# A hybrid Conformer and attention step: attention and convolution put in source order on VectorE and ScalarE, key, value and state loads issued early, first and last transfers in parts

## The chip, the cores and the metric

The kernel runs on one core of one Trainium2 chip. The core has a matmul engine (PE, with its weight loads PEld), a vector engine (DVE), a scalar engine (ACT), GpSimd (POOL), a sync engine (SP) that issues most transfers, and 16 DMA engines that carry them. In the trace each engine takes its instructions in the order in which they stand in the built program; one at the head that waits holds all behind it. The metric is the device time of one execution in microseconds (us), lower is better.

## What is computed

One layer of a streaming encoder, for 256 rows of a new sequence and 8 running streams of 16 rows, 384 rows in all, in float32:

```python
h    = rmsnorm(x, norm_mix_g)
proj = h @ w_in                  # glu | q | k | v | forget logits | gate_a | gate_b
u    = glu_in[..., :D_CONV] * sigmoid(glu_in[..., D_CONV:])
z    = layernorm(causal_dwconv(ext, conv_dw_w, conv_dw_b), conv_ln_g, conv_ln_b)   # 31 taps
a_out = (z * sigmoid(z)) @ conv_pw_out
logf = log_sigmoid(f_logit + b_forget)
b_out = attn_fn(rmsnorm(q, q_norm_g), rmsnorm(k, k_norm_g), v, logf) @ w_att_out   # 8 heads
x    = x + (gate_a * a_out + gate_b * b_out) @ w_out
up   = rmsnorm(x, norm_ffn_g) @ w_up
x    = x + (silu(causal_dwconv(g_half)) * u_half) @ w_down                          # 3 taps
```

The sample streams attend to 128 cached keys and values per head and stream; new keys, values, log gates and convolution states are outputs too.

## The kernel before

**Split matmuls.** Every weight matrix is streamed once from HBM in row pairs (two blocks of 128 rows by 512 columns) into one of three `raw` buffers. ACT casts a pair to `hi` (L148) and DVE forms `lo = raw - hi` (L149); three `hi` and three `lo` buffers exist. A product is then three matmuls, `hi*hi`, `hi*lo` and `lo*hi`. So a new pair can be cast only when PE has used up the pair three before it, and loaded only when the pair three before it has been split.

**Jobs and steps.** `gemm` (L227) runs jobs; a job accumulates over its rows `k` in PSUM, and after the last one its results are taken out by `evac` (L253 to L256). After each `k` it calls `tick`, which advances side generators by one step. A row `k` is called a step here; a pair is used in two steps. In the stage with the GLU columns there are four jobs (`glu_evac(g)`, g = 0 to 3) of 16 steps of 12 matmuls of 384 columns, and two side generators run in it: `attention()` and `conv()`.

**Attention.** For head h the steps are, counted from step 5 + 6h: 1 `head_operands` (DVE transposes the cached keys `kc` into `kTs`, L611, and copies the padded queries `qz`, L617), 4 `head_scores` (PE writes three score tiles s0, s1, s2_; the third needs `kTs` and `qz`, L630; DVE adds the bias and takes maxima, ACT exponentiates), 9 `head_probs` (PE transposes the probabilities into two tiles, taken out by ACT as `pT` and by DVE as `pz`, L653), 12 `head_out` (PE; DVE copies `on`, L665, and `attT`, L670), 14 `head_last` (PE transposes `on`, L675). Their PSUM tiles come from `misc`, three buffers used in turn: s0, s1 and s2_ of the next head stand in the buffers that `head_last`, `pT` and `pz` used just before. Head 2's `head_last` is at step 31, right behind the last matmuls of job 1; head 0's `head_probs` is at step 14, one step before the end of job 0.

**Convolution.** For each of 8 groups of channels, `fill` builds an extended tile and `tap` adds one of 31 taps on DVE (L754), one per step, the groups 17 steps apart. It goes on long after the attention.

**What sets the order.** PE's order is the program's own (`manual_schedule` for PE). On DVE, ACT and SP a scheduler places instructions at build time by its own estimates and by priorities: `tc.high_priority(offset=n)` moves what is inside it n places ahead. Offsets are 150 for the weight splits and their loads (`SPLIT_AHEAD`), 250 for the attention steps (`ATT_AHEAD`), 400 for taking out PSUM results (`EVAC_AHEAD`). `queued` chains an instruction behind the newest chained one of its engine. In the start block (L302) SP, ACT and DVE are in the program's order too.

**Loads around it.** SP issues the cached keys of the next head (`load_k`, L587) after `head_operands`, and biases and values (L592 to L600) after `head_probs`. At the start SP alone issues the rows of x and the first weights, in the order L102, L104, L132, L102, L104, L132, L139. At the end each of the three last output tiles of 128 x 512 is added on DVE (L1052) and stored by SP (L1055).

Of the kernel before, what the change touches and what calls it, by code (L numbers as in the profile page):

```python
# [33 lines left out]
SPLIT_AHEAD, ATT_AHEAD, EVAC_AHEAD = 150, 250, 400  # L34
# [6 lines left out]
def hybrid_step(  # L41
# [36 lines left out]

    mm = nc.tensor.matmul
    tr = nc.tensor.transpose  # L80
    tt = nc.vector.tensor_tensor
    stt = nc.vector.scalar_tensor_tensor
    ts = nc.vector.tensor_scalar
# [15 lines left out]
    def load_x(c, n):  # L99
        cs = slice(c * P, (c + n) * P)  # L100
        o = c % 4 * P
        queued(nc.sync.dma_start(xs[c // 4][:, 0:2, o:o + n * P],  # L102
                                 x_prompt[0, :, cs].rearrange("(t p) d -> p t d", p=P)))
        queued(nc.sync.dma_start(xs[c // 4][:, 2, o:o + n * P], xin[2][:, cs]))  # L104
# [7 lines left out]
    def newton_rsqrt(r, s, m):  # L112
        queued(nc.scalar.activation(s, m, AF.Sqrt), in_first())
        nc.vector.reciprocal(r, s)
# [31 lines left out]
    def split_rows(hi, lo, raw, o, k):  # L146
        first = in_first()
        queued(nc.scalar.copy(hi[:, k, :o], raw[:, k, :o]), first)  # L148
        queued(tt(lo[:, k, :o], raw[:, k, :o], f(hi[:, k, :o]), op=ALU.subtract), first)  # L149

# [76 lines left out]
    def gemm(jobs, sides=(), wide=False):  # L227
        for js in jobs:
# [4 lines left out]
            for j, k in [(j, k + i) for k in range(0, js[0]["nk"], 2) for j in js for i in range(2)]:  # L233
# [29 lines left out]
    def blocks(rows, put):  # L263
        src = rows.rearrange("p t (m b j) -> p b m t j", m=4, b=4)
        for b in range(4):
            for a in range(4):
                nc.vector.transpose(put(a, slice(32 * b, 32 * b + 32)), src[32 * a:32 * a + 32, b])  # L267
# [22 lines left out]
    def x_chunk(c):  # L290
# [5 lines left out]
        with tc.high_priority(offset=EVAC_AHEAD):  # L296
            queued(nc.scalar.activation(hi, ps[:, :NT], AF.Identity, scale=g))  # L297
# [4 lines left out]
    with tc.manual_schedule(engines={ENG.SP, ENG.Activation, ENG.DVE}):  # L302
        nc.vector.memset(junk[:, 0:1], 0.0)
# [18 lines left out]
        nc.vector.tensor_copy(gm[:], pv[:, :16])  # L322
# [3 lines left out]
        warm_up(FILL)  # L326
        split_rows(hi, lo, first, V_COLS[0][0][1], slice(1, 2))
        x_chunk(1)
# [11 lines left out]
    def over_partitions(dg, dst):  # L340
# [3 lines left out]
        nc.scalar.copy(dst, ps[:, :NT])  # L344
# [46 lines left out]
    def small_columns():  # L391
        ps = misc_tile()
        tr(ps[:, :R_N], vrow[:R_N, :], ident[:R_N, :R_N])
        nc.vector.tensor_copy(col[:], ps[:, :R_N])
        ts(qgs[:], col[:, R_QG:R_QG + 1], float(P) ** -0.5, None, op0=ALU.mult)

    def first_norm():
        for c in range(2, 16, 2):
# [6 lines left out]
            if c % 4 == 2:  # L405
                for t in range(NTT):
                    n = c // 4
                    sq = nc.scalar.activation(junk[:], xs[n][:, t, :], AF.Square, accum_out=ssx[:, t, n:n + 1])
# [9 lines left out]
        with tc.high_priority(offset=EVAC_AHEAD):  # L418
            nc.vector.tensor_reduce(mt[:], ssx[:], axis=mybir.AxisListType.X, op=ALU.add)
            ts(mt[:], mt[:], 1.0 / DM, EPS, op0=ALU.mult, op1=ALU.add)  # L420
            r = rsqrt(mt[:], [P, NTT], p_x0, "r1")
            nc.vector.tensor_copy(rs1[:], r[:])
# [14 lines left out]
    def tok_job(dst, c0, n, sq):  # L437
        d = job("B", 16, ha, tok_evac(dst, c0, n))

        def post():  # L440
            for t in range(NTT):
                for h in range(c0 // P, (c0 + n) // P):
                    jk = p_qkv.tile([P, P], F32, tag="jk", bufs=2, name="jk")
                    nc.scalar.activation(jk[:], dst[:, t, h * P:(h + 1) * P], AF.Square,
# [4 lines left out]
    def tok_evac(dst, c0, n, shared=True):  # L449
        def ev(t, ps):  # L450
            if shared and t % 2:
                ts(dst[:, t, c0:c0 + n], ps[:, :n], rs1[:, t:t + 1], None, op0=ALU.mult)
            else:
                queued(nc.scalar.activation(dst[:, t, c0:c0 + n], ps[:, :n], AF.Identity, scale=rs1[:, t:t + 1]),
# [16 lines left out]
    nc.scalar.activation(e[:], e[:], AF.Exp, scale=-1.0)  # L471
    ts(r[:], e[:], 2.0, None, op0=ALU.add)
    nc.vector.reciprocal(r[:], r[:])
# [27 lines left out]
    def bias_rows():  # L501
        for _ in range(6):
            yield
        for i in range(2):
# [3 lines left out]
            nc.vector.tensor_copy(cw[:, i * 124:(i + 1) * 124], ps[:, :124])  # L508
            nc.vector.tensor_copy(fw[:, i * 66:(i + 1) * 66], ps[:, 128:128 + 66])
# [5 lines left out]
        nc.scalar.activation(crow[:, :2 * P], ps[:H, :2 * P], AF.Copy, scale=-1.0)  # L515
        ps = misc_tile()
        mm(ps[:H, :P], lg[:, 2, :], bm[:], start=True, stop=True)
        nc.scalar.activation(crow[:, 2 * P:], ps[:H, :P], AF.Copy, scale=-1.0)
# [3 lines left out]
        nc.scalar.copy(drow[:], ps[:64, :P])  # L522
# [18 lines left out]
    def q_panel(n):  # L541
        blocks(qt[:, :, 512 * n:512 * (n + 1)], by_feature(attT[:, 4 * n:4 * n + 4]))
        for h in range(4 * n, 4 * n + 4):
            nc.scalar.activation(attT[:, h], attT[:, h], AF.Identity, scale=qgs[:])
# [64 lines left out]
    def head_past_keys(d):  # L609
        kTs = p_att.tile([P, 8, P], F32, tag="kTs", bufs=1, name="kTs")  # L610
        nc.vector.transpose(kTs[:].rearrange("p b k -> p (b k)"), kcs[d["h"]][:])  # L611
        d["kTs"] = kTs

    def head_operands(d):
        head_past_keys(d)
        d["bs"] = bss[d["h"]]
        nc.vector.tensor_copy(qz[d["h"] % 2][:, :, :, 0:16], by_stream(attT[:, d["h"], 2 * P:]))  # L617

    def head_scores(d):
# [14 lines left out]
        for i, (sp_, o, n) in enumerate(segs):  # L634
            v = pr[:, o * P:(o + n) * P]
            nc.vector.tensor_tensor_reduce(out=v, in0=sp_[:, :n * P], in1=bs[:, o * P:(o + n) * P], scale=1.0,
                                           scalar=-3.0e38, op0=ALU.add, op1=ALU.max, accum_out=mx[:, i:i + 1])
            ts(mx[:, 3 + i:4 + i], mx[:, i:i + 1], -1.0, None, op0=ALU.mult)
            nc.scalar.activation(v, v, AF.Exp, bias=mx[:, 3 + i:4 + i], accum_out=mx[:, 6 + i:7 + i])
            nc.vector.reciprocal(mx[:, i:i + 1], mx[:, 6 + i:7 + i])  # L640
            nc.scalar.activation(v, v, AF.Identity, scale=mx[:, i:i + 1])
        d["pr"] = pr

    def head_probs(d):
# [5 lines left out]
        nc.scalar.copy(pT[:].rearrange("p a b -> p (a b)"), ps[:])  # L650
        ps = misc_tile()
        tr(ps[:, :P], pr[:, 3 * P:4 * P], ident[:])
        nc.vector.tensor_copy(pz[d["h"] % 2][:, :, :, 0:16], by_stream(ps[:, :P]))  # L653
        d["pT"] = pT

    def head_out(d):
# [8 lines left out]
        nc.vector.tensor_copy(on[:], pn[:, :P])  # L665
# [4 lines left out]
        nc.vector.tensor_copy(attT[:, h, :2 * P], po[:, :2 * P])  # L670
        d["on"] = on

    def head_last(d):
        ps = misc_tile()
        tr(ps[:, :P], d["on"][:], ident[:])  # L675
        nc.vector.tensor_copy(attT[:, d["h"], 2 * P:], ps[:, :P])

    def attention():
        at = {}
        for d in heads:  # L680
            for off, step in ((1, head_operands), (4, head_scores), (9, head_probs),
                              (12, head_out), (14, head_last)):
                at[ATT_FIRST + 6 * d["h"] + off] = step, d
        for t in range(max(at) + 1):
            if t in at:
                step, d = at[t]
                with tc.high_priority(offset=ATT_AHEAD):
                    step(d)
# [418 lines left out]
```

## Time and profile before

| | |
|---|---|
| median of 3 runs | 1998.66 us (1998.60 to 1998.87) |
| the profiled execution's own time | 1998.56 us |
| its span in the profile | 1996.7 us |
| DVE busy | 1305.3 us (65%) |
| ACT busy | 743.2 us (37%) |
| POOL busy | 89.5 us (4%) |
| read from HBM, written | 266.98 MB, 7.86 MB |
| GLU stage with attention, from the first 384-column matmul | 214.6 us on |

The span is counted from the profile's first instruction to its last; the run's own time is 1.9 us longer. A timeline row has start, duration, engine, line, operation, output and inputs, count, and in brackets how long the engine had sat idle before it and what ended that. A matmul's duration runs to its modelled end, so durations of neighbours overlap; PE's pace is read from the distance of two starts.

### The profile page before, as it was taken

The page shows a single profiled execution, that of the slowest core. Times are in us where ns is not written, and L with a number is a line of the kernel's source. Part 1 is how long each engine was busy: PE and PEld are TensorE (multiplying, and loading weights), DVE is VectorE, ACT ScalarE, POOL GpSimd, SP SyncE. Part 2 cuts the span into 40 slices and gives each one's busy share as a digit, 9 for nine tenths or more (in the row PEclk, how much of TensorE's full clock was granted, in tenths as well). Part 3 has the DMA queues.
Part 4 walks back from the last instruction along what each step waited for, and adds up shares of the span by engine and source line. Part 5 has one row for each costly group of instructions (what it writes and reads, how often), then busy time and mean ns, then how long its engine had stood idle before and what let it go on. Part 6 is the DMA issues. An engine that isn't in the chain of part 4 may idle for free.

```text
span 1996.7 us, 24449 instructions
## 1 busy us (share of the span) xinstructions
PE 1986.5 (99%) x9383; PEld 1676.0 (84%) x9383; DVE 1305.3 (65%) x1908; ACT 743.2 (37%) x1077; POOL 89.5 (4%) x216
## 2 busy tenths in 40 slices
PE   9999999999999999999999999999999999999999
PEld 9888999888888888888888888888888888888887
DVE  4455889788755487676867683377673376638663
ACT  5535354433334433344333432233332233323321
POOL 1000011100000000000000000010000000000000
PEclk9999999999999999999999999999999999999999
DMA  6564767444443334534344443444433444343443
GB/s 184 149 188 117 216 154 161 141 140 131 130 129 124 128 125 163 165 122 137 119 137 126 129 134 129 129 126 127 136 129 132 132 118 137 128 133 120 138 158 106
DMA packets 209254, 275.98 MB, mean 138 GB/s; under 512 B 55878, under 2 KB 96729, under 8 KB 209129
## 3 DMA queue, kind: packets, MB, share of 16 engines
q1 hardware_dynamic: 208817, 273.85, 46.0%
q8 instruction: 73, 1.20, 0.3%
q0 software_dynamic: 288, 0.57, 0.1%
q14 instruction: 44, 0.36, 0.1%
q10 hardware_dynamic: 32, 0.01, 0.0%
HBM read 266.98 MB, written 7.86 MB: 138 GB/s over the span
## 4 chain that ended last, share of the span: by engine, by line
PE 96%; DVE 2%; DMA 1%; issue 0%; SPq 0%; ACT 0%; DVEq 0%; ACTq 0%
PE acc L252 20%; PE acc L250 20%; PE acc L251 20%; PE misc L252 10%; PE misc L251 10%; PE misc L250 10%; PE acc L245 2%; PE acc L247 2%; PE acc L246 2%; DVE lo L149 1%; DMA raw<-in_w_in_dram 0%; DVE mixT L267 0%; DVE ut L754 0%; DMA vc<-in_cache_v_dram 0%; DMA bs<-c_dr 0%
## 5 line engine op out<-in xcount | busy, mean ns | idle before, releaser
L149 DVE TENSOR_TENSOR lo<-raw,hi 128x1024 fp32r<-128x1024 f32 (+2 forms) x481 | 580.5, 1207 | 530.7 <-ACT hi L148 526.8
L148 ACT CAST hi<-raw 128x1024 fp32r<-128x1024 f32 (+2 forms) x481 | 496.3, 1032 | 970.1 <-PE misc L252 841.1
L250 PE MATMUL acc<-hi,xg 128*128 128x512 f32 x704 | 274.9, 390 | 0.0
L252 PE MATMUL acc<-hi,xg 128*128 128x512 f32 x704 | 273.9, 389 | 0.0
L251 PE MATMUL acc<-lo,xg 128*128 128x512 f32 x704 | 273.9, 389 | 0.0
L250 PE MATMUL acc<-hi,hT 128*128 128x512 f32 (+1 forms) x512 | 193.0, 377 | 0.5 <-ACT hT L297 0.5
L252 PE MATMUL acc<-hi,hT 128*128 128x512 f32 (+1 forms) x512 | 190.4, 372 | 0.2
L251 PE MATMUL acc<-lo,hT 128*128 128x512 f32 (+1 forms) x512 | 190.3, 372 | 0.0
L250 PEld LDWEIGHTS acc<-hi,xg 128*128 128x128 f32 x704 | 132.1, 188 | 28.4
L754 DVE SCALAR_TENSOR_TENSOR ut<-ext,cw,ut 128x384 f32<-128x384 f32 x240 | 151.9, 633 | 6.0
L252 PEld LDWEIGHTS acc<-hi,xg 128*128 128x128 f32 x704 | 132.1, 188 | 27.5
L251 PEld LDWEIGHTS acc<-lo,xg 128*128 128x128 f32 x704 | 132.2, 188 | 27.1
L252 PE MATMUL misc<-hi,xg 128*128 128x512 f32 x352 | 137.0, 389 | 0.0
L250 PE MATMUL misc<-hi,xg 128*128 128x512 f32 x352 | 137.0, 389 | 0.0
L251 PE MATMUL misc<-lo,xg 128*128 128x512 f32 x352 | 136.9, 389 | 0.0
L250 PE MATMUL acc<-hi,act 128*128 128x512 f32 x352 | 136.9, 389 | 0.0
L251 PE MATMUL acc<-lo,act 128*128 128x512 f32 x352 | 136.9, 389 | 0.0
L252 PE MATMUL acc<-hi,act 128*128 128x512 f32 x352 | 136.9, 389 | 0.0
L267 DVE STREAM_TRANSPOSE extf<-tok 32x384 f32<-32x384 f32 x176 | 100.3, 570 | 30.9 <-ACT tok L988 28.2
L267 DVE STREAM_TRANSPOSE uT<-tok 32x384 f32<-32x384 f32 x176 | 100.3, 570 | 29.7 <-ACT tok L988 26.9
L250 PEld LDWEIGHTS acc<-hi,hT 128*128 128x128 f32 x512 | 96.2, 188 | 16.1 <-ACT hT L297 1.0
L252 PEld LDWEIGHTS acc<-hi,hT 128*128 128x128 f32 x512 | 96.1, 188 | 15.7 <-DVE hT L298 0.7
(325 smaller groups left out, 3133.8 us busy)
## 6 DMA issues: line engine op xcount, KB each, us to landing
raw<-in_w_up_dram SPq DMA_DIRECT2D x176, 512.0 KB
raw<-in_w_in_dram SPq DMA_DIRECT2D x96, 512.0 KB
raw<-in_w_down_dram SPq DMA_DIRECT2D x88, 512.0 KB
raw<-in_w_in_dram SPq DMA_DIRECT2D x64, 256.0 KB
raw<-in_w_out_dram SPq DMA_DIRECT2D x32, 512.0 KB
raw<-in_w_att_out_dram SPq DMA_DIRECT2D x16, 512.0 KB
raw<-in_conv_pw_out_dram SPq DMA_DIRECT2D x16, 512.0 KB
raw<-in_w_in_dram SPq DMA_DIRECT2D x23, 344.0 KB
```

The costliest lines, as they stand in the source:

```text
L148: queued(nc.scalar.copy(hi[:, k, :o], raw[:, k, :o]), first)
L149: queued(tt(lo[:, k, :o], raw[:, k, :o], f(hi[:, k, :o]), op=ALU.subtract), first)
L245: mm(o, hi[:, kk, s], ah, start=st, stop=False)
L246: mm(o, hi[:, kk, s], al, start=False, stop=False)
L247: mm(o, lo[:, kk, s], ah, start=False, stop=sp)
L250: mm(o, ah[:, s], hi[:, kk, :n], start=st, stop=False)
L251: mm(o, ah[:, s], lo[:, kk, :n], start=False, stop=False)
L252: mm(o, al[:, s], hi[:, kk, :n], start=False, stop=sp)
L267: nc.vector.transpose(put(a, slice(32 * b, 32 * b + 32)), src[32 * a:32 * a + 32, b])
L754: stt(o, v, wc, o, op0=ALU.mult, op1=ALU.add)
```

## The change

All instructions of DVE and ACT that the kernel issues go through a wrapper, `InOrder`. While the list `chained` holds something, each of them is chained behind the one issued before it on its engine. The list is filled just before the GLU jobs and cleared after them. Weight splits and the taking-out of PSUM results empty it while they issue, so they stay outside the chain and are placed by the scheduler as before. The attention steps no longer have a priority of their own. Scaling the probabilities becomes a step of its own, with one reciprocal of 128x3 in place of three of 128x1. Keys are loaded two heads ahead and, with biases, values and convolution states, issued at the priority of the weight loads. At the start the sample rows of x go to ACT's queue, ahead of the norm weights, and chunk 1 of x is taken before the second half of the first weight pair. The last output tile is added and stored in two halves, the second from ACT's queue.

```diff
-SPLIT_AHEAD, ATT_AHEAD, EVAC_AHEAD = 150, 250, 400
+SPLIT_AHEAD, EVAC_AHEAD = 150, 400
...
+    chained = []
+
+    class InOrder:
+        def __init__(self, eng):
+            self.eng = eng
+
+        def __getattr__(self, name):
+            op = getattr(self.eng, name)
+
+            def call(*a, **kw):
+                d = op(*a, **kw)
+                if chained:
+                    queued(d)
+                return d
+            return call
+
+    dve, act = InOrder(nc.vector), InOrder(nc.scalar)
...
-    def load_x(c, n):
+    def load_x(c, n, sample=nc.sync):
...
-        queued(nc.sync.dma_start(xs[c // 4][:, 2, o:o + n * P], xin[2][:, cs]))
+        queued(sample.dma_start(xs[c // 4][:, 2, o:o + n * P], xin[2][:, cs]))
...
     def split_rows(hi, lo, raw, o, k):
         first = in_first()
-        queued(nc.scalar.copy(hi[:, k, :o], raw[:, k, :o]), first)
+        held, chained[:] = chained[:], []
+        queued(act.copy(hi[:, k, :o], raw[:, k, :o]), first)
         queued(tt(lo[:, k, :o], raw[:, k, :o], f(hi[:, k, :o]), op=ALU.subtract), first)
+        chained[:] = held
...
                 if sp:
+                    held, chained[:] = chained[:], []
                     with tc.high_priority(offset=EVAC_AHEAD):
-                        for m in range(nb):
+                        for m in range(len(ps)):
                             j["evac"](m, ps[m])
+                    chained[:] = held
...
+        load_x(0, 1, nc.scalar)
         nc.scalar.dma_start(gm_row[:], norm_mix_g[0].rearrange("(c p) -> c p", p=P))
-        nc.scalar.activation(junk[:, 1:2], junk[:, 0:1], AF.Identity)
-        load_x(0, 1)
         first = stream_tile()
         fetch_row(first, plan[0], 0)
-        load_x(1, 1)
+        load_x(1, 1, nc.scalar)
+        act.activation(junk[:, 1:2], junk[:, 0:1], AF.Identity)
...
         warm_up(FILL)
+        x_chunk(1)
         split_rows(hi, lo, first, V_COLS[0][0][1], slice(1, 2))
-        x_chunk(1)
...
-            nc.scalar.activation(v, v, AF.Exp, bias=mx[:, 3 + i:4 + i], accum_out=mx[:, 6 + i:7 + i])
-            nc.vector.reciprocal(mx[:, i:i + 1], mx[:, 6 + i:7 + i])
-            nc.scalar.activation(v, v, AF.Identity, scale=mx[:, i:i + 1])
-        d["pr"] = pr
+            act.activation(v, v, AF.Exp, bias=mx[:, 3 + i:4 + i], accum_out=mx[:, 6 + i:7 + i])
+        d["pr"], d["mx"], d["segs"] = pr, mx, segs
+
+    def head_scale(d):
+        pr, mx = d["pr"], d["mx"]
+        dve.reciprocal(mx[:, 0:3], mx[:, 6:9])
+        for i, (_, o, n) in enumerate(d["segs"]):
+            v = pr[:, o * P:(o + n) * P]
+            act.activation(v, v, AF.Identity, scale=mx[:, i:i + 1])
...
+    def next_keys(d):
+        with tc.high_priority(offset=SPLIT_AHEAD):
+            if d["h"] + 2 < H:
+                load_k(d["h"] + 2)
+
+    def next_rest(d):
+        with tc.high_priority(offset=SPLIT_AHEAD):
+            if d["h"] + 2 < H:
+                load_b(d["h"] + 2)
+            if 0 < d["h"] < H - 1:
+                load_v(d["h"] + 1)
...
-            for off, step in ((1, head_operands), (4, head_scores), (9, head_probs),
-                              (12, head_out), (14, head_last)):
-                at[ATT_FIRST + 6 * d["h"] + off] = step, d
+            for off, step in ((1, head_operands), (3, next_keys), (4, head_scores), (5, head_scale), (8, next_rest),
+                              (9, head_probs), (12, head_out), (14, head_last)):
+                at.setdefault(ATT_FIRST + 6 * d["h"] + off, []).append((step, d))
...
-                with tc.high_priority(offset=ATT_AHEAD):
-                    step(d)
-                if step is head_operands and d["h"] + 1 < H:
-                    load_k(d["h"] + 1)
...
                 if w == -16:
-                    load_state(c)
+                    with tc.high_priority(offset=SPLIT_AHEAD):
+                        load_state(c)
...
     load_k(0)
     load_b(0)
+    load_k(1)
     load_v(0)
...
     att_steps = attention()
+    chained.append(True)
     gemm([job("A", 16, ha, glu_evac(g)) for g in range(4)], [att_steps, conv_steps])
     drain(att_steps)
+    chained.clear()
...
-                tt(ys, ps[:], ys, op=ALU.add)
-                if last:
-                    dst = [y_prompt[0, 0:P], y_prompt[0, P:2 * P], y_sample.rearrange("b t d -> (b t) d")][t]
-                    nc.sync.dma_start(dst[:, n * 512:(n + 1) * 512], ys)
+                parts = [(0, 512)] if not last or n < 3 or t < 2 else [(0, 256), (256, 256)]
+                for o, w in parts:
+                    tt(ys[:, o:o + w], ps[:, o:o + w], ys[:, o:o + w], op=ALU.add)
+                    if last:
+                        dst = [y_prompt[0, 0:P], y_prompt[0, P:2 * P], y_sample.rearrange("b t d -> (b t) d")][t]
+                        (nc.scalar if o else nc.sync).dma_start(dst[:, n * 512 + o:n * 512 + o + w], ys[:, o:o + w])
```

PE's instructions and their order are the same before and after. Because of the wrapper, DVE and ACT instructions all carry its line, L89, in the changed program. What moves is shown at three places of DVE's order; numbers behind names tell tiles and buffers apart.

**The end of job 1.** Before, `on` of head 2 and the split `lo_2809` stand ahead of the four instructions (`sgb`, then `ut` from `acc`) that take out job 1:

```order
L665 COPY on_2797<-misc_2787 128x128
L149 TENSOR_TENSOR lo_2809<-raw_2805,hi_2808 128x1024
L670 COPY attT_150<-misc_2799 128x256
L754 SCALAR_TENSOR_TENSOR ut_1998<-ext_2561,cw_753,ut_1998 128x384 x2
L706 TENSOR_TENSOR sgb_2845<-acc_2386,rs1b_146 128x384
L706 TENSOR_TENSOR sgb_2848<-acc_2387,rs1b_146 128x384
L710 TENSOR_TENSOR ut_1998<-acc_2388,rs1b_146 128x384
L710 TENSOR_TENSOR ut_1998<-acc_2389,rs1b_146 128x384
L676 COPY attT_150<-misc_2855 128x128
```

and in the changed program:

```order
L89 TENSOR_TENSOR sgb_2837<-acc_2383,rs1b_146 128x384
L89 TENSOR_TENSOR sgb_2840<-acc_2384,rs1b_146 128x384
L89 TENSOR_TENSOR ut_1998<-acc_2385,rs1b_146 128x384
L89 TENSOR_TENSOR ut_1998<-acc_2386,rs1b_146 128x384
L89 TENSOR_TENSOR lo_2752<-raw_2748,hi_2751 128x1024
L89 RECIPROCAL mx_2737<-mx_2737 128x3
L89 SCALAR_TENSOR_TENSOR ut_1998<-ext_2556,cw_753,ut_1998 128x384
L89 COPY on_2794<-misc_2784 128x128
L89 COPY attT_150<-misc_2796 128x256
L89 SCALAR_TENSOR_TENSOR ut_1998<-ext_2556,cw_753,ut_1998 128x384
L89 TENSOR_TENSOR lo_2806<-raw_2802,hi_2805 128x1024
L89 STREAM_TRANSPOSE kTs_2821<-kc_2514 128x1024
```

The four now stand ahead of a split (`lo_2752`, of the pair that job 2 begins with), of head 3's reciprocal, of a tap and of `on`. On ACT the `hi` cast of the same pair stands behind the two sigmoids of job 1.

**The end of job 0.** Before, `pz0` of head 0 and the splits are ahead of the four that take out job 0:

```order
L149 TENSOR_TENSOR lo_2262<-raw_2258,hi_2261 128x1024
L149 TENSOR_TENSOR lo_2301<-raw_2297,hi_2300 128x1024
L653 COPY pz0_1992<-misc_2323 128x8x16
L706 TENSOR_TENSOR sgb_2345<-acc_2025,rs1b_146 128x384
L706 TENSOR_TENSOR sgb_2348<-acc_2026,rs1b_146 128x384
L710 TENSOR_TENSOR ut_1998<-acc_2027,rs1b_146 128x384
L710 TENSOR_TENSOR ut_1998<-acc_2028,rs1b_146 128x384
```

and in the changed program:

```order
L89 TENSOR_TENSOR sgb_2348<-acc_2030,rs1b_146 128x384
L89 TENSOR_TENSOR sgb_2351<-acc_2031,rs1b_146 128x384
L89 TENSOR_TENSOR ut_1998<-acc_2032,rs1b_146 128x384
L89 TENSOR_TENSOR ut_1998<-acc_2033,rs1b_146 128x384
L89 TENSOR_TENSOR lo_2306<-raw_2302,hi_2305 128x1024
L89 COPY pz0_1992<-misc_2328 128x8x16
```

`pz0` moved behind the four and behind one split.

**The keys of head 7.** Before, `kTs` of head 7 stands behind a split:

```order
L653 COPY pz0_1992<-misc_3457 128x8x16
L754 SCALAR_TENSOR_TENSOR ut_1998<-ext_3079,cw_753,ut_1998 128x384
L149 TENSOR_TENSOR lo_3513<-raw_3509,hi_3512 128x1024
L611 STREAM_TRANSPOSE kTs_3409<-kc_3211 128x1024
L731 STREAM_TRANSPOSE ext_3598<-sc_2000 128x8x32
```

and in the changed program:

```order
L89 COPY on_3363<-misc_3353 128x128
L89 TENSOR_TENSOR lo_3380<-raw_3376,hi_3379 128x1024
L89 COPY attT_150<-misc_3365 128x256
L89 SCALAR_TENSOR_TENSOR ut_1998<-ext_2556,cw_753,ut_1998 128x384
L89 SCALAR_TENSOR_TENSOR ut_1998<-ext_3074,cw_753,ut_1998 128x384
L89 STREAM_TRANSPOSE kTs_3395<-kc_3068 128x1024
L89 TENSOR_TENSOR lo_3423<-raw_3419,hi_3422 128x1024
L89 COPY qz1_1991<-attT_150 128x8x16
```

`kTs` of head 7 moved ahead of the split, to its own step, 48, three steps before the scores at step 51. Head 0's `kTs` and `qz`, made before at 105.19 us and 167.64 us, now stand in the place of a transpose of `ext` (L731), behind the last transpose of the new keys (L267) and directly ahead of PE's scores of head 0, which need them.

More of the change, by code (lines that the diff above doesn't have):

```diff
@@ L266, in blocks @@
             for a in range(4):
-                nc.vector.transpose(put(a, slice(32 * b, 32 * b + 32)), src[32 * a:32 * a + 32, b])
+                dve.transpose(put(a, slice(32 * b, 32 * b + 32)), src[32 * a:32 * a + 32, b])
     def by_feature(dst):
@@ L610, in head_past_keys @@
         kTs = p_att.tile([P, 8, P], F32, tag="kTs", bufs=1, name="kTs")
-        nc.vector.transpose(kTs[:].rearrange("p b k -> p (b k)"), kcs[d["h"]][:])
+        dve.transpose(kTs[:].rearrange("p b k -> p (b k)"), kcs[d["h"]][:])
         d["kTs"] = kTs
@@ L793, in hybrid_step @@
         hi, lo = aHL[h // 4][:, 0, h % 4, :], aHL[h // 4][:, 1, h % 4, :]
-        nc.scalar.copy(hi, attT[:, h, :])
+        act.copy(hi, attT[:, h, :])
         tt(lo, attT[:, h, :], f(hi), op=ALU.subtract)
@@ L813, in layer_norm @@
         mm(ps[:, :NT], avg[:], sm[:], start=True, stop=True)
-        nc.scalar.copy(mu, ps[:, :NT])
+        act.copy(mu, ps[:, :NT])
         yield
@@ L975, in hybrid_step @@
                           state_ffn[0].rearrange("b r (c a d) -> a (b r) c d", a=4, d=32)[a])
-    after(8, lambda: nc.vector.transpose(sfT[:], sfr[:]))
+    after(8, lambda: dve.transpose(sfT[:], sfr[:]))
     extf = p_f.tile([P, 4, 24, 18], F32, name="extf")
```

112 lines of the change are left out of this document (54 added, 58 removed).

## The prediction

> **What bounds the kernel now.** I read the page's busy times first, then who PE waits for, then busy times by stretches of 50 us.
>
> ```profile
> PE 1986.5 (99%) x9383; PEld 1676.0 (84%) x9383; DVE 1305.3 (65%) x1908; ACT 743.2 (37%) x1077; POOL 89.5 (4%) x216
> ```
> ```profile
> PE misc L630 <- DVE kTs L611: 2.5, 1, 2.5
> ```
> ```profile
> 350.00:400.00 50.00, 47.50 (x289) 43.70 (x288) 39.81 (x72) 21.79 (x38) 4.68 (x8) 0.97 0.49 145
> 1950.00:2000.00 50.00, 42.29 (x187) 34.70 (x185) 13.91 (x14) 8.40 (x8) 0.00 (x0) 0.97 0.28 95
> ```
>
> PE is busy from the first microseconds to the last; its matmuls are the same afterwards, in the same order. So the change is worth only what it does to PE's gaps: the start, one wait of 2.5 us, and the 4.4 us between the last matmul and the end. The stretch from 350 us also has a price that is not idle time: its clock column (the third from the end) is 0.97. Timeline and finer stretches show both:
>
> ```profile
> 349.72 1.04 ACT L148 CAST hi<-raw 128x1024 fp32r<-128x1024 f32 x1 [1.47 <-PE acc L246]
> 350.80 1.22 DVE L149 TENSOR_TENSOR lo<-raw,hi 128x1024 fp32r<-128x1024 f32 x1 [1.26 <-ACT hi L148]
> 351.94 1.24 DVE L611 STREAM_TRANSPOSE kTs<-kc 128x1024 f32<-128x1024 f32 x1
> 353.23 0.64 PE L630 MATMUL misc<-kTs,qz 128*32 128x128 f32 x16 [2.50 <-DVE kTs L611]
> ```
> ```profile
> 354.20:354.60 0.40, 0.40 (x4) 0.40 (x3) 0.40 (x4) 0.40 (x1) 0.00 (x0) 0.74 1.08 374
> 355.00:356.00 1.00, 1.00 (x4) 1.00 (x4) 0.11 (x1) 0.99 (x4) 0.00 (x0) 0.50 0.91 295
> 357.40:357.80 0.40, 0.40 (x3) 0.40 (x2) 0.00 (x0) 0.00 (x0) 0.00 (x0) 0.50 0.52 115
> 357.80:358.20 0.40, 0.40 (x4) 0.40 (x3) 0.00 (x0) 0.00 (x0) 0.00 (x0) 1.00 0.28 57
> ```
>
> The keys of head 7 are late because of DVE's order, not of a load: a split stands ahead of them, it waits for its cast, and the cast waits until PE gives a buffer back. Soon after the wait the granted clock is 0.50 from about 354.4 to 357.8 us, 3.4 us, which costs half of that, 1.7 us.
>
> **The change part by part.** *Head 7 (gain).* `kTs` now stands at step 48, ahead of the split; by the order it can end about 4 us before PE's scores need it. The wait and its half clock go: -2.5 and -1.7, together -4.2 us.
>
> *Head 0 (loss).* `kTs` and `qz` of head 0 now come behind the last transpose of the new keys.
>
> ```profile
> 234.75 0.57 DVE L267 STREAM_TRANSPOSE qt<-kt 32x384 f32<-32x384 f32 x1
> 235.36 0.45 DVE L731 STREAM_TRANSPOSE ext<-sc 128x256 f32<-128x256 f32 x1
> 240.42 0.21 DVE L617 COPY qz<-attT 128x128 f32<-128x128 f32 x1
> 236.40 0.65 PE L630 MATMUL misc<-kTs,qz 128*32 128x128 f32 x16
> ```
>
> They take the place of the `ext` transpose at 235.36: 1.2 (the kTs row) and 0.2 make 236.8, and PE wants them at 236.4: +0.4 us. DVE has no idle time ahead of it there, so nothing hides it.
>
> *Job 1 (loss, the largest).* Taking out a job's results is outside the chain and has the highest priority, while `on`, the reciprocal and the taps are chained in source order. In the built order the four instructions that take out job 1 come first, though their data come last. DVE will stand at them until PE ends job 1, and behind them wait the split of job 2's first pair, head 3's reciprocal, a tap and `on` of head 2. PE's very next instruction is `head_last` of head 2, which needs `on`. Before, `on` was long done:
>
> ```profile
> 293.68 1.08 DVE L706 TENSOR_TENSOR sgb<-acc,rs1b 128x384 f32<-128x384 f32 x2 [0.41 <-PE acc L247]
> 294.72 1.08 DVE L710 TENSOR_TENSOR ut<-acc,rs1b 128x384 f32<-128x384 f32 x2
> 294.27 1.05 ACT L707 ACTIVATE sgb<-sgb 128x384 f32<-128x384 f32 x2 [2.27 <-DVE sgb L706]
> 295.22 1.03 ACT L148 CAST hi<-raw 128x1024 fp32r<-128x1024 f32 x1
> 295.04 0.27 PE L675 MATMUL misc<-ident,on 128*128 128x128 f32 x1
> 302.79 1.21 DVE L149 TENSOR_TENSOR lo<-raw,hi 128x1024 fp32r<-128x1024 f32 x1
> 303.92 0.16 DVE L640 RECIPROCAL mx<-mx 128x1 f32<-128x1 f32 x1
> 304.18 0.61 DVE L754 SCALAR_TENSOR_TENSOR ut<-ext,cw,ut 128x384 f32<-128x384 f32 x1
> 306.77 0.29 DVE L665 COPY on<-misc 128x128 f32<-128x128 f32 x1 [0.67 <-PE misc L663]
> ```
>
> On these times: the sigmoids end at 295.3, the cast that follows them on ACT at 296.3. The split starts then and takes 1.2 (297.5), the reciprocal 0.15, the tap 0.55 net of overlap, `on` 0.25: 298.4. PE arrives at 295.0 and waits 3.4 us. Even without `on`, PE's next matmuls need that split, so 2.4 us of it would stand. Behind it I followed DVE, ACT and PE on to the next job with the same rows: the next keys, `qz` and probabilities come 0 to 3 us early, so no further wait is charged. A wait longer than the 2.5 us one should bring the half clock again: +1.7. Its bounds are 0, if the wait falls on two of the 3.4 us stretches and neither is idle enough, and 3.4, if both are.
>
> The Trainium skill, TensorE: Matmul & The Clock Gate, Part 1 (The HAM clock gate), says that the clock drops to half after an idle stretch of a free-running window of about 3.4 us. The trace agrees on the length (354.4 to 357.8) but not on the need of a whole idle window, since 2.5 us were enough. By the rule as written the new wait would cost no clock and the sum would end 1.7 us lower.
>
> *Job 0 (loss).* Here `pz` of head 0 stands behind the four and a split. PE's third score tile of head 1 (L626) reuses the buffer that this `pz` copy empties.
>
> ```profile
> 248.23 0.29 DVE L653 COPY pz<-misc 128x128 f32<-128x128 f32 x1
> 248.77 1.10 DVE L706 TENSOR_TENSOR sgb<-acc,rs1b 128x384 f32<-128x384 f32 x2 [0.24 <-PE acc L247]
> 249.83 1.08 DVE L710 TENSOR_TENSOR ut<-acc,rs1b 128x384 f32<-128x384 f32 x2
> 250.81 0.38 PE L626 MATMUL misc<-qt,attT 128*128 128x128 f32 x2
> ```
>
> Before, `pz` was copied at 248.23. Now the four end at 250.85 net, the split adds 1.15, `pz` 0.2, the semaphore under 0.1: 252.2 against PE's 250.8, +1.4 us. For its clock the nearest rows are the 2.5 us wait (half clock) and the gaps of the start (0.46 us at 8.36, clock 1.00): I take 0, with 1.7 as the other end. At the end of job 2 only taps and a reciprocal are passed by; its `on` is wanted two steps (4 us) later, so I cost it at nothing; without that cover it would be the 3.4 us again.
>
> *Loads, reciprocals, taps.* Early loads find SP idle and PE never waits for weights in this stage: nothing. Sixteen fewer reciprocals of 0.15 us lie on DVE beside PE: nothing.
>
> *Start (gain).* Two issues of 0.47 us leave SP's queue, so the weights' issues come 0.5 and 1.0 us earlier.
>
> ```profile
> 2.00:4.00 2.00, 2.00 (x11) 1.78 (x10) 0.00 (x0) 0.78 (x2) 2.00 (x5) 1.00 0.75 205
> 4.00:6.00 2.00, 2.00 (x11) 1.96 (x11) 0.86 (x3) 0.96 (x2) 2.00 (x5) 1.00 0.88 222
> ```
> ```profile
> 2.79 0.47 SPq L104 DMA_DIRECT2D xs<-in_x_sample_dram  x1
> 7.34 0.48 ACT L148 CAST hi<-raw 128x344 fp32r<-128x344 f32 x1 [1.58 <-DMA raw<-in_w_in_dram]
> 8.36 0.42 PE L250 MATMUL acc<-hi,hT 128*128 128x344 f32 x1 [0.46 <-ACT hT L297]
> 12.92 0.77 ACT L148 CAST hi<-raw 128x688 fp32r<-128x688 f32 x1 [3.70 <-DMA raw<-in_w_in_dram]
> ```
>
> Taking chunk 1 of x ahead of the weight half frees PE's wait at 8.36 (0.4 to 0.75 us), but a few microseconds later PE depends on transfers that land around 12 us (ACT waits 3.70 us for one), and the DMA engines are 0.75 to 0.88 busy. The bytes are the same, so only the idle quarter of 2 to 4 us, 0.5 us, can be won: -0.4, between -1.0 (the full two issues) and +0.4 (the norm weights now second in ACT's queue).
>
> The Trainium skill, DMA: Bandwidth & Descriptors, Issuing engines are not separate DMA queues, says that issuing from several engines saves only the sequencer's time, since all share the 16 engines; the busy shares above agree, and by it the sum would be 0.4 us higher.
>
> *End.* Halving the last tile can start its first store earlier, but the engines are full with the two stores before it:
>
> ```profile
> 1992.33 0.69 DVE L1052 TENSOR_TENSOR y<-misc,y 128x512 f32<-128x512 f32 x1
> 1993.60:1994.00 0.40, 0.00 (x0) 0.00 (x0) 0.00 (x0) 0.00 (x0) 0.00 (x0) 1.00 1.08 379
> 1994.40:1994.80 0.40, 0.00 (x0) 0.00 (x0) 0.00 (x0) 0.00 (x0) 0.00 (x0) 1.00 0.77 266
> ```
>
> 768 KB at 375 GB/s is 2.1 us in either form: 0, between -0.3 (half the tile's add) and +0.3 (smaller pieces).
>
> **Sum.** -4.2 + 0.4 + 3.4 + 1.7 + 1.4 - 0.4 + 0 = +2.3 us. The profiled execution took 1998.56 us (span 1996.7), 0.1 under the median: 2000.9 us. One wait goes and a longer one comes.
>
> **The rivals.**
> - *Half clock after every wait (slower).* If 41% idle in a 3.4 us stretch (1.4 us) is enough, job 0's wait costs 1.7 more and job 1's wait, spread over two stretches, another 1.7: 2004.3. It decides from a threshold between the 16% that the start shows without a drop (0.5 us idle in 3.4) and the 66% (2.2 us of the wait lie in 351.0 to 354.4) that gave one. 0.17.
> - *Weights late behind held keys (slower).* SP issues head 6's keys only after head 4's `kTs`, now at 301.6, and the weights queue behind them. By the rows the split they feed is done 0.6 to 2.2 us before PE needs what follows it; if a landing is 2 us later, a wait of 2 us and its half clock come: 2004.6. Against it: no wait for weights here before. 0.10.
> - *No half clock after job 1's wait.* It falls about evenly on two stretches: 1999.2. This is also the time by the skill's clock rule. 0.15.
> - *The new waits are covered (faster).* If PE reached those places late for another reason, or DVE did not stand at the four, only -4.2 + 0.4 - 0.4 stays: 1994.4. For it: DVE is 65% busy. Against: the order is fixed, and PE has nothing between the end of job 1 and `head_last`. 0.10.
> - *The change does not lift head 7's wait:* 2005.1. Against: `kTs` stands three steps ahead. 0.03.
>
> **How the numbers follow.** The forecast has 0.45, its own range 1999.6 to 2002.4. The 0.8 range leaves out the faster case and the last one, and takes in the clock's bounds: 1997.6 to 2004.6. About 0.2%, 4.0 us, is what a measurement of this kernel can tell from no change: the forecast and the third rival lie within (0.60), the first two and the last above it (0.30), the fourth below (0.10).
>
> **What would show it.** Right: no wait of PE for `kTs` of head 7; PE waiting about 3.4 us for `on` at the first matmul behind job 1, near 295 us, with clock 0.5 for 3.4 us after it; 1.4 us at the third score tile of head 1, near 251; 0.4 at head 0's scores; DVE idle for some 7 us before job 1 is taken out. Wrong: no idle PE near 295 (then the time falls to about 1994 to 1996), a clock of 0.5 near 253, or a wait for weights after 300. A start that gains more than 1 us, or an end more than 0.3 us shorter, would mean that I put too much weight on the DMA engines' share.

## The result, and the profile after

The changed kernel takes 2004.8 us (median of 6 runs, 2003.07 to 2005.4) against 1998.36 us of the kernel before on the same chip (6 runs, 1996.59 to 1998.87). The ratio is 1.0034, with a 95% interval from 1.0021 to 1.0046: 0.3% slower, clear of the noise. The profiled executions have spans of 2003.3 and 1996.7 us, 6.6 us apart; that of the changed kernel took 2005.2 us.

The list of what PE waits for, in the changed kernel (line, what it waits for; us in total, times, longest). Three entries of 1.5, 0.5 and 0.2 us that the kernel before has too are left out:

```profile
PE misc L701 <- DVE on L89: 4.0, 1, 4.0
PE misc L647 <- DVE pz L89: 2.1, 1, 2.1
PE misc L364 <- DVE ln L89: 0.4, 1, 0.4
PE misc L770 <- DVE attT L89: 0.4, 1, 0.4
PE acc L270 <- DVE lo L89: 0.3, 1, 0.3
PE misc L651 <- DVE qz L89: 0.3, 1, 0.3
```

The wait for head 7's `kTs` is gone. Those of 4.0 and 2.1 us are new, at the two places that the prediction named. As PE's order is the same in both kernels, each matmul has a counterpart, and the difference of their starts shows term by term where the time went (times are those of the kernel before, minus is earlier; "half clock" is a stretch with a granted clock of 0.50):

| place | difference of PE's starts | term | predicted |
|---|---|---|---|
| start, to 25 us | 0 to -1.7 | -1.7 | -0.4 |
| head 0's scores | -1.7 to -1.3 | +0.3 | +0.4 |
| job 0, wait for `pz` | -1.3 to +0.9 | +2.2 | +1.4 |
| job 0, half clock behind it | +0.9 to +2.5 | +1.6 | 0 |
| job 1, wait for `on` | +2.5 to +6.7 | +4.2 | +3.4 |
| job 1, half clock behind it | +6.7 to +9.0 | +2.3 | +1.7 |
| 314 to 318 us, `fill` and the scores of head 5 | +9.0 to +9.95 | +0.9 | 0 |
| head 7, wait and half clock | +9.95 to +6.1 | -3.8 | -4.2 |
| layer norm, 643 us | +6.1 to +6.4 | +0.3 | 0 |
| from the last matmul to the end | +6.4 to +6.6 | +0.2 | 0 |

Timeline of job 1's end in the changed kernel (start, duration, engine; in brackets the idle time before and what ended it):

```profile
296.21 1.08 DVE L89 TENSOR_TENSOR sgb<-acc,rs1b 128x384 f32<-128x384 f32 x2 [7.34 <-PE acc L266]
296.80 1.10 ACT L89 ACTIVATE sgb<-sgb 128x384 f32<-128x384 f32 x2 [6.52 <-DVE sgb L89]
297.81 1.03 ACT L89 CAST hi<-raw 128x1024 fp32r<-128x1024 f32 x1
298.87 1.23 DVE L89 TENSOR_TENSOR lo<-raw,hi 128x1024 fp32r<-128x1024 f32 x1 [0.54 <-ACT hi L89]
300.02 0.17 DVE L89 RECIPROCAL mx<-mx 128x3 f32<-128x3 f32 x1
300.10 1.26 DVE L89 SCALAR_TENSOR_TENSOR ut<-ext,cw,ut 128x384 f32<-128x384 f32 x1
301.29 0.28 DVE L89 COPY on<-misc 128x128 f32<-128x128 f32 x1
301.71 0.45 PE L701 MATMUL misc<-ident,on 128*128 128x128 f32 x1 [3.98 <-DVE on L89]
```

DVE stands idle for 7.34 us in front of the four instructions that take out job 1; then come the split, the reciprocal, the tap and `on`, and PE waits for all of it. This is the chain that the prediction walked. One row is longer than it said: the tap takes 1.26 us, not 0.6. Job 0 shows the same:

```profile
247.42 1.10 DVE L89 TENSOR_TENSOR sgb<-acc,rs1b 128x384 f32<-128x384 f32 x2 [3.27 <-PE acc L266]
249.28 2.93 POOL L741 TENSOR_TENSOR ut<-ut,sgb 128x384 f32<-128x384 f32 x2 [3.26 <-ACT sgb L89]
249.47 1.89 DVE L89 TENSOR_TENSOR lo<-raw,hi 128x1024 fp32r<-128x1024 f32 x1
251.28 0.28 DVE L89 COPY pz<-misc 128x128 f32<-128x128 f32 x1
251.71 0.46 PE L647 MATMUL misc<-qt,attT 128*128 128x128 f32 x2 [2.09 <-DVE pz L89]
```

The split takes 1.89 us where 1.2 is usual, while POOL multiplies `ut` by the sigmoids. The clock behind both waits, in stretches laid on its own steps (start and end, length, then PE's busy time in the stretch; third from the end the granted clock):

```profile
248.79:252.20 3.41, 1.32 (x11) 0.82 (x14) 3.38 (x8) 2.32 (x4) 2.92 (x2) 1.00 0.87 284
252.20:255.61 3.41, 3.41 (x24) 3.03 (x25) 0.93 (x7) 2.42 (x7) 0.02 (x1) 0.50 0.08 16
255.61:259.03 3.42, 3.42 (x28) 3.30 (x30) 1.22 (x2) 0.46 (x1) 0.00 (x0) 1.00 0.74 219
```
```profile
296.57:299.99 3.42, 1.17 (x7) 0.85 (x5) 2.88 (x5) 1.98 (x3) 2.04 (x2) 1.00 0.01 3
299.99:303.40 3.41, 1.69 (x6) 1.72 (x7) 3.41 (x7) 3.08 (x5) 2.75 (x3) 0.50 0.28 77
303.40:306.81 3.41, 3.41 (x15) 3.31 (x13) 3.41 (x6) 0.00 (x0) 0.00 (x0) 0.50 0.21 33
306.81:310.23 3.42, 3.42 (x32) 3.25 (x34) 2.13 (x8) 2.12 (x3) 0.00 (x0) 1.00 1.24 177
```

One stretch at half clock follows job 0's wait, and two follow job 1's. The start, in the stretches whose rows before stand in the prediction, and the cast that waits for its weights:

```profile
2.00:4.00 2.00, 2.00 (x11) 1.78 (x10) 0.00 (x0) 1.55 (x3) 2.00 (x5) 1.00 0.91 274
4.00:6.00 2.00, 2.00 (x11) 1.96 (x11) 0.93 (x3) 1.00 (x2) 2.00 (x5) 1.00 0.92 240
```
```profile
10.58 0.77 ACT L89 CAST hi<-raw 128x688 fp32r<-128x688 f32 x1 [2.05 <-DMA raw<-in_w_in_dram]
```

The cast that began at 12.92 us now begins at 10.58.

### The profile page after: what moved, and what is told of

Its sections match the earlier page's. It is cut to its first block, busy times and chain, and to the rows that moved or that the text cites. A ratio compares the mean times of both kernels' runs of the same rounds, so it can differ in the third digit from the quotient of the medians.

```text
span 2003.3 us, 24449 instructions
## 1 busy us (share of the span) xinstructions
PE 1988.8 (99%) x9383; PEld 1677.8 (84%) x9383; DVE 1302.7 (65%) x1893; ACT 741.8 (37%) x1077; POOL 90.5 (5%) x216
## 4 chain that ended last, share of the span: by engine, by line
PE 96%; DVE 3%; issue 0%; ACT 0%; DVEq 0%; POOL 0%; ACTq 0%; POOLq 0%
PE acc L271 20%; PE acc L270 20%; PE acc L269 20%; PE misc L271 10%; PE misc L270 10%; PE misc L269 10%; PE acc L264 2%; PE acc L265 2%; PE acc L266 2%; DVE lo L89 1%; DVE qt L89 0%; DVE mixT L89 0%; DVE sgA L89 0%; PE misc L314 0%; PE misc L651 0%
## 5 line engine op out<-in xcount | busy, mean ns | idle before, releaser
L89 DVE TENSOR_TENSOR lo<-raw,hi 128x1024 fp32r<-128x1024 f32 (+2 forms) x481 | 580.0, 1206 | 527.7 <-ACT hi L89 523.8
L89 ACT CAST hi<-raw 128x1024 fp32r<-128x1024 f32 (+2 forms) x481 | 496.0, 1031 | 958.5 <-PE misc L271 834.0
L89 DVE SCALAR_TENSOR_TENSOR ut<-ext,cw,ut 128x384 f32<-128x384 f32 x240 | 147.9, 634 | 3.7
L89 DVE STREAM_TRANSPOSE extf<-tok 32x384 f32<-32x384 f32 x176 | 100.3, 570 | 30.9 <-ACT tok L89 28.2
L89 DVE STREAM_TRANSPOSE uT<-tok 32x384 f32<-32x384 f32 x176 | 100.3, 570 | 29.7 <-ACT tok L89 26.9
L270 PEld LDWEIGHTS acc<-lo,hT 128*128 128x128 f32 x512 | 96.2, 188 | 15.5 <-DVE lo L89 0.6
L269 PEld LDWEIGHTS acc<-hi,hT 128*128 128x128 f32 x512 | 96.3, 188 | 15.1 <-issue 0.2
```

Source lines behind the costliest of these rows:

```text
L89: d = op(*a, **kw)
L269: mm(o, ah[:, s], hi[:, kk, :n], start=st, stop=False)
L270: mm(o, ah[:, s], lo[:, kk, :n], start=False, stop=False)
```

## Experiments

Times are medians; each ratio is to the kernel before on the same chip. "Lag" is the difference of PE's starts from the kernel before in the profiled executions, as in the table above.

**Both jobs taken out behind attention's copies (att_first).** An instruction that takes out a job gets an order-only dependence (it fixes the built order and adds no wait) on the newest copies of the attention steps, `pz` and `attT`; `on` stands directly ahead of that `attT`:

```diff
+        mark("att", dve.tensor_copy(pz[...], by_stream(ps[:, :P])))
...
+        mark("att", dve.tensor_copy(attT[:, h, :2 * P], po[:, :2 * P]))
...
+                elif held_back:
+                    for n in behind.get(d.ins.engine, {}).values():
+                        tc.add_manual_dep(d.ins, n, ...)
```

> The changed kernel with one edit: the four instructions that take out a GLU job are placed behind the newest copy of an attention step (pz, or on and attT) on DVE. Theory (they stood ahead of pz and on): both waits and both half clocks go, 2.1 + 1.6 at job 0 and 4.0 + 2.4 at job 1, so 2004.8 falls by about 10 to 1994 to 1995.5. Rival 1 (weights late behind held keys): on is in time, but PE now waits for the split of job 2's first pair or later weights by 2 us or more with half clock, 1998 to 2001. Rival 2 (the waits come from DVE being slowed, not from its order): both waits stay above 1 us, 2001 to 2004.

It took 1998.88 us, ratio 1.0007 (0.9998 to 1.0016): 5.9 us better than the change, not 10. The two waits were gone: the lag stood at -1.3 from head 0 to 300 us. Then it rose by 3.4 for two new waits and by 3.0 for half clock. Neither wait was for weights, so the time lies in the first rival's range for another reason. The profiled execution took 2000.4 us, the highest of 11; two others took 1997.4 and 1997.5 us at a mean clock of 1.000, so what half clock costs here differs between executions. PE's rows and DVE's behind job 1:

```profile
300.69 0.70 PE L656 MATMUL misc<-qt,attT 128*128 128x256 f32 x2 [1.67 <-DVE attT L90]
302.64 0.77 PE L658 MATMUL misc<-qt,attT 128*128 128x128 f32 x2 [1.26 <-DVE pz L90]
```
```profile
292.38 1.08 DVE L90 TENSOR_TENSOR sgb<-acc,rs1b 128x384 f32<-128x384 f32 x2 [2.18 <-PE acc L275]
294.42 1.81 DVE L90 TENSOR_TENSOR lo<-raw,hi 128x1024 fp32r<-128x1024 f32 x1
297.43 1.23 DVE L90 STREAM_TRANSPOSE kTs<-kc 128x1024 f32<-128x1024 f32 x1
300.36 0.27 DVE L90 COPY attT<-misc 128x128 f32<-128x128 f32 x1
```

From 292.4 us DVE works without a pause, and the copy that empties a tile for head 4's scores comes only at 300.36. In the kernel before, head 4's `kTs` and this copy are at

```profile
286.39 1.24 DVE L611 STREAM_TRANSPOSE kTs<-kc 128x1024 f32<-128x1024 f32 x1
295.72 0.28 DVE L676 COPY attT<-misc 128x128 f32<-128x128 f32 x1
```

the keys some 7 us ahead of job 1's end, and the copy right behind its taking-out. So source order costs in two ways: it lets DVE idle ahead of the job's end and puts all that it could have done there behind it. In the changed kernel this second lateness was covered, because PE was already late: its list has no wait at head 4's scores.

**Job 1 alone (on_first).** The mark on `pz` is left out.

> The same edit for the copies of head_out alone, so that only job 1 is taken out behind on, and job 0 is left as in the changed kernel. Theory: job 0's wait of 2.1 us and its half clock stay, job 1's 4.0 and 2.4 go: about 1998.4. Rival 1 (weights late): 2001 to 2003. If the price of one wait moves to the other, the difference from the run with both edits is not 3.7 us.

2003.0 us, ratio 1.0021 (1.0012 to 1.0030); expected 1998.4. Job 0's terms stayed as in the change (+2.2 and +1.6). Job 1's 4.2 and 2.3 went, and 3.4 for waits and 1.6 for half clock came at head 4's scores. Taking one wait away was worth 1.8 us, because the next one stood behind it.

**POOL's product on DVE (gate_on_dve).**

```diff
-                nc.gpsimd.tensor_tensor(u, u, sgb[m - 2][:], op=ALU.mult)
+                s = sgb[m - 2]
+                after(2, lambda: dve.tensor_tensor(u, u, s[:], op=ALU.mult))
```

> The changed kernel, with the product of ut and the sigmoids done by DVE two steps later instead of by POOL at once. Theory (the order sets the waits, POOL's work beside DVE only lengthens them: a split of 1.89 instead of 1.2 us at job 0, a tap of 1.26 instead of 0.6 at job 1): waits of about 1.4 and 3.4 us. If 41% idle of a clock stretch is enough for the half clock, both half clocks stay and the time falls by 1.3 to about 2003.5; if it is not enough, job 0's goes too and the time is about 2002. Rival (DVE being slowed is the cause of the waits): both under 0.7 us, 1996 to 1998.

2001.19 us, ratio 1.0017 (1.0008 to 1.0026), below both values expected. The rows of DVE, and job 0's stretches:

```profile
249.45 1.22 DVE L89 TENSOR_TENSOR lo<-raw,hi 128x1024 fp32r<-128x1024 f32 x1
297.80 0.59 DVE L89 SCALAR_TENSOR_TENSOR ut<-ext,cw,ut 128x384 f32<-128x384 f32 x1
```
```profile
247.38:250.79 3.41, 2.22 (x13) 1.81 (x12) 3.40 (x7) 3.38 (x4) 0.00 (x0) 1.00 1.22 277
250.79:254.21 3.42, 3.19 (x31) 2.90 (x32) 1.52 (x10) 2.52 (x8) 0.00 (x0) 1.00 0.20 69
```

Split and tap are back at 1.22 and 0.59 us, and the waits at 1.42 and 3.24, the predicted 1.4 and 3.4. Job 0's wait gives no half clock now, and job 1's gives one stretch instead of two. The DMA engines' share during the split is 1.09 in both kernels, so transfers are not what had slowed it. POOL's work beside DVE cost 1.4 us of waiting, and that pushed two more stretches to half clock.

**The clock by itself (clock_probe).** The kernel before, with waits of chosen length in the feed-forward stage:

```diff
+        with tc.high_priority(offset=2 * EVAC_AHEAD):
+            nc.vector.tensor_copy(probe_t[0][:], ps[:, :64])
+            for i in range(n):
+                nc.vector.tensor_copy(probe_t[1 - i % 2][:], probe_t[i % 2][:])
...
+                mm(js[0]["ps"][0][:64, :P], probe["due"][:], ident[:], start=True, stop=True)
```

> The kernel before with a chain of 1 to 19 small DVE copies at the end of each feed-forward job; PE's next matmul (an extra one, into a tile that is then overwritten) reads its result, so PE stands for some 0.4 to 4 us, some 60 us apart. Read from it: the idle share of each 3.4 us clock stretch and the clock granted in the next. Theory (half idle is the bound): no half clock below about 45% idle, always above about 55%, whatever the length of the wait, so waits of 1.7 to 3.4 us give it or not by where they fall. Rival 1 (a whole stretch must be idle): only waits over 3.4 us give it. Rival 2 (a bound near 20 to 40%): waits of 1.0 us already give it now and then.

One run, 2161.05 us, with 26 waits of 0.56 to 7.16 us. All drops of the clock lie on one grid with a period of 3.413 us, to within 0.003 us. Stretches on this grid:

```profile
1862.84:1866.25 3.41, 1.59 (x8) 0.97 (x6) 3.03 (x8) 1.04 (x1) 0.00 (x0) 1.00 0.54 154
1866.25:1869.66 3.41, 2.27 (x10) 1.80 (x11) 1.01 (x4) 0.00 (x0) 0.00 (x0) 1.00 0.49 143
1869.66:1873.08 3.42, 3.42 (x16) 2.82 (x16) 0.00 (x0) 0.91 (x1) 0.00 (x0) 1.00 0.05 16
...
2122.25:2125.66 3.41, 1.21 (x6) 0.67 (x4) 3.30 (x8) 1.04 (x1) 0.00 (x0) 1.00 0.76 229
2125.66:2129.07 3.41, 2.88 (x7) 2.11 (x8) 0.44 (x3) 0.00 (x0) 0.00 (x0) 0.50 0.76 269
2129.07:2132.49 3.42, 3.42 (x9) 2.64 (x8) 0.00 (x0) 0.00 (x0) 0.00 (x0) 0.50 0.11 41
...
1838.94:1842.36 3.42, 1.37 (x7) 0.79 (x5) 3.26 (x8) 1.04 (x1) 0.00 (x0) 1.00 0.46 153
1845.77:1849.18 3.41, 3.16 (x8) 2.35 (x9) 0.19 (x1) 0.00 (x0) 0.00 (x0) 0.50 0.00 1
2094.94:2098.35 3.41, 2.99 (x8) 2.18 (x9) 0.34 (x2) 0.00 (x0) 0.00 (x0) 0.50 0.25 83
```

A wait of 2.96 us, from 1864.43 on, left 47% and 67% busy in its two stretches and cost no clock. One of 2.73 us, from 2123.45 on, left 35% busy in the first, and two stretches at half clock followed. At full clock, stretches with 47% (1.59 us) and more busy kept it, and those with 40% (1.37 us) and less lost it in the next one. Behind head 7's wait in start_chunk, the run of one start edit below, a stretch with 43% lost it too:

```profile
351.15:354.56 3.41, 1.45 (x21) 1.26 (x22) 3.31 (x11) 1.17 (x3) 1.14 (x2) 1.00 1.02 316
```

So the bound lies between 43% and 47%, near the half that was expected. At half clock, 88% busy (2.99 us) did not bring full clock back, 93% (3.16 us) did. Both rivals fell: no stretch need be idle altogether, and the waits of 0.56 to 1.80 us in this kernel cost no clock. For waits between 2 and 3 us, what counts is where they fall on the grid.

**The start edits alone (start_only), and each of them (start_queue, start_chunk).** In the first all start edits of the diff stand in the kernel before. The second has the queue edit without the exchange of `x_chunk(1)` and `split_rows`, the third has that exchange alone.

> The kernel before with the start edits alone (sample rows of x from ACT's queue, chunk 1 of x ahead of the second half of the first weight pair). Theory: PE reaches the end of the first job about 1.6 us earlier and nothing takes it back: 1996.8. Rival (the gain is taken back by a later wait, or came from another part of the change): within 0.4 us of before.

> The kernel before with the queue edit of the start alone: two rows of x go to ACT's queue, chunk 1 of x stays behind the second half of the first weight pair. Read from where PE's matmuls stand at 22 us against the kernel before. Theory (the third weight pair is issued about 2 us earlier, and the DMA engines can move more in the first 10 us than their busy share suggests): 1.0 to 1.5 us earlier. Rival (the gain comes from PE's order and ACT's at 8 us): under 0.4 us.

> The kernel before with the other start edit alone: chunk 1 of x is taken ahead of the second half of the first weight pair. Theory: PE reaches 10 us some 0.2 to 0.7 us earlier and then stands for the third pair as before, so at 22 us it is within 0.3 us. Rival: 1.0 us or more earlier at 22 us.

start_only took 1996.73 us, ratio 0.9991 (0.9982 to 0.9999), as expected. Its lag of -1.7 us lasts to 349 us. In that execution head 7's wait of 2.5 us fell on two stretches and gave no half clock. The lag at 25 us was -1.7 with the queue edit and -0.1 with the exchange alone. Single runs took 1995.14 and 1998.69 us, beside 1998.65 of the kernel before; 1.6 us of the first one's distance is head 7's half clock, which that execution didn't have. The gain is the queue edit's.

**The last tile in halves alone (tail_only).**

> The kernel before with the last output tile in two halves alone. Theory (the end is bound by the DMA engines' share for 768 KB, not by the first store's start): within 0.3 us of before, and the same distance from the last matmul to the end. Rival (the halves shorten the end): 0.5 us or more faster.

1997.73 us, ratio 1.0001 (0.9992 to 1.0010): no difference. From the start of the last matmul to the end are 5.00 to 5.02 us in six profiles with the halves, and 4.69 to 4.91 in five without (clock_probe, with its added work at the end, is not counted): the halves cost 0.1 to 0.3 us.

**Head 7's keys by an exchange of two neighbours on DVE (start_key7).** The start edits, and one order-only dependence: the second split issued behind head 7's `kTs` has to stand behind it.

```diff
+        if d["h"] == H - 1:
+            last_keys.append(t_.ins.name)
...
+        for name in behind_keys[:1]:
+            tc.add_manual_dep(t_.ins, name, ...)
```

> The kernel before with the start edits, and on DVE two neighbouring instructions exchanged: kTs of head 7 ahead of the split that stood before it. Theory (head 7's wait is DVE's order alone): PE's wait for kTs goes, 2.5 us and the half clock in those executions that had it, so from 1996.7 to 1993 to 1994, and the executions spread less. Rival 1 (kTs is late for another reason, its load or its buffer): 1996.7 stays. Rival 2 (the split is what PE needs next): the wait moves to it, 1995 to 1996.5.

1992.89 us (1992.75 to 1993.17 in 11 runs), ratio 0.9977 (0.9969 to 0.9986). It beats both kernels. In the traces DVE's order differs from start_only in this exchange alone. What PE waits for, all of it, and the stretch from 350 us:

```profile
PE misc L325 <- POOL ident L109: 1.5, 1, 1.5
PE misc L894 <- DVE sgA L888: 0.5, 2, 0.3
PE misc L529 <- ACT crow L523: 0.2, 1, 0.2
```
```profile
350.00:400.00 50.00, 50.00 (x294) 45.55 (x293) 42.32 (x78) 22.82 (x41) 5.28 (x8) 1.00 0.52 149
```

PE is busy there all the time at full clock. Two neighbours exchanged are worth 3.8 us by the medians, 1996.73 less 1992.89; the two were taken on two chips, and each against the kernel before on its own chip gives 3.6. The executions now agree within 0.4 us. The kernel before spread over 3.3 us, from 1996.42 at a mean clock of 1.000 to 1999.77 at 0.998. That fits a wait that falls differently on the grid from execution to execution; of these two no trace was kept.

**Two copies out of the chain (last_free).** att_first, and the copies of `head_last` and `head_probs` issued outside the chain:

```diff
+    def free_copy(dst, src):
+        with tc.high_priority(offset=250):
+            return nc.vector.tensor_copy(dst, src)
```

> The run with both jobs taken out behind the attention copies (att_first), and the copies of head_last and head_probs outside the chain, at the priority of 250 that attention had before; on DVE attT of head 2 then stands right behind the taking-out of job 1, and pz of head 3 ahead of a split. Theory (DVE has 11 us of work in a row behind job 1, and copies that PE waits for stand at its end): the waits of 1.7 and 1.3 us for them at 300 go, and one of 1.0 to 1.5 us for qz takes their place, without or with little half clock: from 1998.9 to 1995 to 1997. Rival 1 (the copies were the only thing late): 1994 to 1994.8. Rival 2 (the wait only moves to the splits that now come later): 1998 to 1999.5.

1994.84 us, ratio 0.9984 (0.9975 to 0.9993). The copy of head 2 and PE's only wait left there:

```profile
294.46 0.28 DVE L102 COPY attT<-misc 128x128 f32<-128x128 f32 x1
300.40 0.21 DVE L90 COPY qz<-attT 128x128 f32<-128x128 f32 x1
```
```profile
PE misc L666 <- DVE qz L90: 1.0, 2, 0.8
```

The copy comes 5.9 us earlier than in att_first. A wait of 0.8 us for `qz` takes the place of the two, without half clock. So DVE's order accounts for the loss: with these copies put ahead, the changed kernel is 10 us faster than as it stood. It stays 2 us behind start_key7.

## Why the prediction was wrong

The direction, both new waits, head 7's gain and head 0's loss were right. The time was outside the range by 0.2 us and 3.9 us above the forecast. By the profiles the sum came out at +6.6 instead of +2.3: job 0 missed 2.4, job 1 1.4, and the waits charged at nothing 1.2. The start, mis-sized the other way, hid 1.3 of this by luck.

- **Head 7 and head 0:** right, -3.8 and +0.3 against -4.2 and +0.4. That head 7's wait was DVE's order alone is shown by start_key7.
- **Job 0, the step that cost most:** "the split adds 1.15" took the split's usual duration. At that place POOL multiplies beside it, and it took 1.89. The wait became 2.1 us instead of 1.4, left 39% busy in its stretch, and so brought the half clock that was costed at 0. With the wait sized 0.7 too small, the step missed 2.4 us. gate_on_dve shows that a wait of 1.4 us costs no clock. The warning stood in the profile of before, in the taps beside POOL's product:

```profile
295.42 2.31 POOL L711 TENSOR_TENSOR ut<-ut,sgb 128x384 f32<-128x384 f32 x2 [4.75 <-ACT sgb L707]
295.91 2.88 DVE L754 SCALAR_TENSOR_TENSOR ut<-ext,cw,ut 128x384 f32<-128x384 f32 x3
```

0.96 us for each of three taps, against 0.61 alone. How much of the half clock comes is in part chance: two of the six executions took 2003.07 and 2003.27 us, inside the range, at a mean clock of 0.999 against 0.997 in the profiled one. No trace of them was kept.

- **Job 1:** the mechanism was right, the size 0.8 short for the same reason. "The half clock again: +1.7" counted one stretch; the wait reached into a second one, which was half busy, and the clock stayed down for two (+2.3).
- **The start:** "only the idle quarter of 2 to 4 us can be won" was wrong, and its bound of -1.0 too. A busy share of 0.75 to 0.88 was taken as if the engines moved all they could. With the issues closer together they moved 274 and 240 GB/s where it had been 205 and 222, at shares of 0.91 and 0.92, and the weights' cast began 2.3 us earlier. Why the landing gains more than the 1.0 us of the issue was not tried.
- **"No further wait is charged" behind job 1:** 0.9 us came at 314 to 318, where PE waits 0.4 us for a copy of `attT` (the rest is in no entry of the list), and 0.3 at the layer norm, where it waits 0.4 us for `ln`.
- **The end:** +0.2, within its bounds, on the loss side.
- **The rivals:** half clock after each wait happened, but the rival's reason, that 1.4 us is enough, fell. Weights behind held keys: no such wait appeared (the 0.3 us for `lo` in the list is at 8.5 us, in the start). The other three did not come: half clock followed job 1's wait, DVE stood at the four for 7.34 us, and head 7's wait went. Against the clock rule of the Trainium skill, TensorE: Matmul & The Clock Gate, Part 1 (The HAM clock gate), which asks for one idle window of about 3.4 us: the runs agree on 3.413 us and on a grid that runs by itself, but a stretch with up to 43% busy already loses the clock.

## What to carry to other kernels

Where the engine in front is 99% busy, price a moved instruction by what runs beside it at its new place, not by its mean; and follow the next waits behind the one removed, since a late engine covers them. Source order on a helper engine also forbids it to work ahead, so first look for the single pair of neighbours to exchange. A wait near 2 us costs nearly twice its length when it leaves one clock stretch less than about 45% busy (job 0: 2.2 and 1.6 us), so shortening it by 0.7 us can be worth 2.

## What was not expected of the hardware

The granted clock falls and returns at different shares. It fell behind a stretch with 43% busy or less and not at 47%, and it came back only behind one with 93% or more; in att_first 92% (3.15 of 3.41 us) still kept it down. The profile models the ends of matmuls, so these shares are not exact. DVE instructions that read two tensors slowed beside POOL's two-tensor product, 1.22 to 1.89 us and 0.59 to 1.26. The Trainium skill, GPSIMD Engine Reference, 1. Specifications, says that POOL shares its SBUF interfaces with DVE and that instructions with two SBUF inputs contend, and gate_on_dve agrees.
